# Reordering the hand-written entry of a one-core mixer-trunk kernel

## Chip, core and metric

The kernel runs on one core of one Trainium2 chip. The metric is device time in microseconds (us) of one execution. The core has five engines, each of which takes its own instructions in order: TensorE (PE) multiplies matrices, VectorE (DVE), ScalarE (ACT) and GpSimd (POOL) work elementwise, and SyncE (SP) here only issues DMAs. Matmuls write to PSUM, of which the kernel uses eight banks of 128 x 512 float32; in this kernel DVE and ACT read and write it, and POOL works on SBUF alone.

## The reference

One layer over 1024 positions of width 1024, in float32:

```
h = rmsnorm(x) * norm_g ;  p = h @ w_in            # w_in: 1024 x 6656
u,v,z_a, x_b,b_g,c_g,z_b, x_c,z_c, g_a,g_b,g_c = split(p)
a = gelu(u) * (chunkwise causal mix of layernorm(gelu(v))) * silu(z_a)
b = b_g * conv3(c_g * x_b) * silu(z_b)
c = (multi-scale causal mean of x_c - x_c) @ w_pool * pool_scale * silu(z_c)
m = sigmoid(g_a) * (a @ w_pa) + sigmoid(g_b) * (b @ w_pb) + sigmoid(g_c) * (c @ w_pc)
out = rmsnorm(x + m @ w_o) * final_g
```

## The kernel before

**Precision.** Every float32 operand of a matmul is split in two: `hi` is the operand rounded by an ACT copy (names end in h, or ch for weights), `lo` is the rest, by a subtraction on DVE or POOL (S1l, cl). A product is three matmuls per 128 rows: hi·hi, hi·lo, lo·hi (`mm3`).

**Seven products for eight.** After the entry, the projection runs over pairs of weight units. h (transposed) is cut in four blocks A11, A12, A21, A22, a pair of units in B11, B12, B21, B22, and each pair costs seven products of 12 matmuls instead of eight:

```
PRODUCTS = (("A11", "B11"), ("A12", "B21"), ("S2", "T2"), ("S3", "T3"),
            ("S1", "T1"), ("A22", "T4"), ("S4", "B22"))
```

S1 = A21 + A22, S2 = S1 - A11, S3 = A11 - A21, S4 = A12 - S2 are made once, in the entry. T1 = B12 - B11, T2 = B22 - T1, T3 = B22 - B12, T4 = B21 - T2 are made for each pair, on DVE into a PSUM bank. A "step" n is one product; `prep(n)` makes its T (if it has one) and its ch and cl. Steps 0 to 3 are the *early products* A11·B11 and A12·B21 of pairs 0 and 1; steps 4 to 8 are S1·T1, S2·T2, S3·T3, A22·T4 and S4·B22 of pair 0; step 9 begins pair 1. A result tile of step n is p with the number n. A product begins by preparing weights up to `AHEAD = 6` steps ahead. From pair 2 on a part of every second pair is done by a further level of the same scheme (`joint`, tiles T_j and cj), whose left side `cut_again` makes from A12 during pair 0.

**The entry** (from line 482) computes the mean squares of x (`squares`, `sums`, `power`, and `newton`, called `roots`), the columns v of the projection from x that is not yet normalised (`project_v`, eight rows i of 24 matmuls each over k), `gelu_v` with the root as a scale, and then the normalised blocks A and S. `as_row` transposes the roots on PE, so that `scaled` can multiply x by them. Rows 0 to 3 of v are computed k by k, since the weights are still arriving; rows 4 to 7 one after the other. `gelu_v` also writes gv to DRAM; `stats_v(i)` takes its mean and variance by bn_stats on DVE, from gv itself or (`again`) from a copy gw reloaded by SP.

**What sets the order.** The entry stands in a block of manual schedule: there PE, ACT, DVE and POOL run its lines in the order in which they are written. All that follows is ordered by the compiler's list planner, with the order of the program as priority and its own costs; it may put instructions from behind the block between its lines. Slots are handed out per tag, eight PSUM banks (`ps`), three of `T` (gv, gw, T_j), 18 of `wc` (ch, cl and the weights of v), four of `raw`; a tile waits until the slot's last tile was read. `keep_s1(p)` copies the first early product of pair p out of PSUM on ACT, `first_o0(p)` adds that to the second early product on DVE and runs a sigmoid on ACT, and both free a bank. p4 (S1·T1) is given a bank after T1 to T4 of pair 0 and T1, T2 of pair 1. S4·B22 is accumulated onto p4 and so waits until DVE has read p4 (u2, u3, o1 in the main loop).

Of the kernel before, what the change touches and what calls it, by code (L numbers as in the profile page):

```python
# [18 lines left out]
KH = KT // 2  # L19
# [42 lines left out]
def hybrid_layer(ctx: ExitStack, tc: tile.TileContext, x, xt, units, ws, wpool, small, rows, out):  # L62
# [128 lines left out]
    def x_lo(half, kk):  # L191
        for c in range(2):
            k = kk + KH * c
            hi, lo = (z[:, kk, :] for z in hb[XB[2 * half + c]])
            nc.vector.scalar_tensor_tensor(out=lo, in0=xs[half, kk][c], scalar=ng[:, k:k + 1], in1=hi.bitcast(F32),
                                           op0=ALU.mult, op1=ALU.subtract)
# [29 lines left out]
    def roots(half):  # L226
        newton(*root[half], norms[:, 1, KH * half:KH * half + KH])

    def as_row(half):
        for i in range(KH):  # L230
            e = KH * half + i
            nc.tensor.transpose(out=B[6 + half][:, tsl(i)], in_=norms[:, 1, e:e + 1].to_broadcast([P, P]), identity=ident)
# [19 lines left out]
    def project_v(i, k, terms=range(3)):  # L252
        hi, lo = (z[:, k % KH, tsl(i % KH)] for z in hb[XB[2 * (i // KH) + k // KH]])
        w = wv[k]
        for e in terms:
            nc.tensor.matmul(pv[i], lhsT=(hi, hi, lo)[e], rhs=(w[0], w[1], w[0])[e], start=k == 0 and e == 0,
                             stop=k == KT - 1 and e == 2)

    def gelu_v(i):
        gvs[i] = slot("T", f"gv{i}", (P, CW))  # L260
        nc.scalar.activation(out=gvs[i], in_=pv[i], func=AF.Gelu_apprx_tanh, scale=norms[:, 1, i:i + 1])
        nc.sync.dma_start(out=v_dram[:, i, :], in_=gvs[i])
# [47 lines left out]
            raw[u] = slot("raw", f"raw{u}", (P, 2, HALF))  # L310
            nc.sync.dma_start(out=raw[u], in_=units[u])

    def prep(n):
        kind, p, r = steps[n]
        name = PRODUCTS[r][1]
        u0, u1 = pairs[p][2]
        load_raw(u0)
        if kind == "n":
            load_raw(u1)
            b = {"B11": raw[u0][:, 0, :], "B21": raw[u0][:, 1, :], "B12": raw[u1][:, 0, :], "B22": raw[u1][:, 1, :]}  # L320
        else:
            v0 = pairs[p + 1][2][0]
            load_raw(v0)
            b = {"B11": raw[u0][:, 1, 0:256], "B21": raw[u0][:, 1, 256:], "B12": raw[v0][:, 1, 0:256],
                 "B22": raw[v0][:, 1, 256:]}

        def add(name, i0, i1, into=None):
            if kind == "n":
                t = bank(f"{name}_{kind}{p}")
            else:  # L330
                t = slot("T", f"{name}_{kind}{p}", (P, HALF)) if into is None else into
            if kind == "j" and into is None:
                T[kind, p, name, "rest"] = t[:, 256:]
                t = t[:, 0:256]
            tt(nc.vector if kind == "n" else nc.gpsimd, t, b[i0] if i0 in b else T[kind, p, i0], b[i1] if i1 in b else T[kind, p, i1], ALU.subtract)
            T[kind, p, name] = t

        if r == 4 and kind == "n":
            add("T1", "B12", "B11")
        elif r == 2:  # L340
            if kind == "j":
                add("T1", "B12", "B11")
            add("T2", "B22", "T1", T["j", p, "T1", "rest"] if kind == "j" else None)
        elif r == 3:
            add("T3", "B22", "B12")
        elif r == 5:
            add("T4", "B21", "T2", T["j", p, "T3", "rest"] if kind == "j" else None)
        if kind == "n":
            hi = slot("wc", f"ch{n}", (P, HALF), F32R)
            lo = slot("wc", f"cl{n}", (P, HALF), F32R)  # L350
            if name in b:
                split_to(hi, lo, b[name], nc.gpsimd)
            else:
                split_to(hi, lo, T[kind, p, name])
            comb[n] = (hi, lo)
        elif r == 0:
            hi = slot("wc", f"ch{n}", (P, HALF), F32R)
            lo = slot("wc", f"cl{n}", (P, HALF), F32R)
            split_to(hi, lo, raw[u0][:, 1, :])
            comb[n] = (hi[:, 0:256], lo[:, 0:256])  # L360
            comb[steps.index(("j", p, 1))] = (hi[:, 256:], lo[:, 256:])
        elif r > 1:
            w = slot("wc", f"cj{n}", (P, 2, 256), F32R)
            split_to(w[:, 0, :], w[:, 1, :], b[name] if name in b else T[kind, p, name])
            comb[n] = (w[:, 0, :], w[:, 1, :])
# [116 lines left out]
    with tc.manual_schedule(engines={ET.PE, ET.Activation, ET.DVE, ET.Pool}):  # L482
        x_hi(0, 0)
        w_hi(0)
        x_lo(0, 0)
        w_lo(0)
        w_lo(4)
        squares(0, 0)
        x_hi(0, 1)
        x_lo(0, 1)  # L490
        w_hi(1)
        w_lo(1)
        w_lo(5)
        squares(0, 1)
        x_hi(0, 2)
        x_lo(0, 2)
        squares(0, 2)
        squares(0, 3)
        w_hi(2)
        x_hi(0, 3)  # L500
        w_hi(3)
        w_lo(2)
        for e in range(3):
            for i in range(KH):
                project_v(i, 0, [e])
        for k in (4, 1):
            for i in range(KH):
                project_v(i, k)
        for i in range(2):
            project_v(i, 5)  # L510
        sums(0)
        w_lo(6)
        w_lo(3)
        w_lo(7)
        x_lo(0, 3)
        roots(0)
        for i in range(2, KH):
            project_v(i, 5)
        for i in range(KH):
            project_v(i, 2)  # L520
        as_row(0)
        for kk in range(KH):
            squares(1, kk)
        for kk in range(KH):
            x_hi(1, kk)
        for i in range(KH):
            project_v(i, 6)
        for i in range(KH):
            project_v(i, 3)
        sums(1)  # L530
        for kk in range(2):
            x_lo(1, kk)
        roots(1)
        for kk in range(2, KH):
            x_lo(1, kk)
        for i in range(KH):
            project_v(i, 7)
            if i == 2:
                as_row(1)
        prep(0)  # L540
        for i in range(KH):
            gelu_v(i)
        for kk in range(KH):
            scaled(0, kk)
            split_h(kk, ("A11", "A12"))
        for k in KORDER:
            project_v(4, k)
        gelu_v(4)
        for kk in range(KH):
            scaled(1, kk)  # L550
        for k in KORDER:
            project_v(5, k)
        gelu_v(5)
        for i in range(6, NT):
            for k in KORDER:
                project_v(i, k)
        f11, f12 = ([xs[0, kk][c] for kk in range(KH)] for c in range(2))
        f21, f22 = ([xs[1, kk][c] for kk in range(KH)] for c in range(2))
        for kk in range(KH):
            s1_, s2_ = (B[6 + c - 2 * (kk % 2)] for c in range(2))  # L560
            tt(nc.vector, s1_, f21[kk], f22[kk], ALU.add)
            tt(nc.vector, s2_, s1_, f11[kk], ALU.subtract)
            tt(nc.vector, f12[kk], f12[kk], s2_, ALU.subtract)
            split_s("S1", kk, s1_)
            split_s("S2", kk, s2_)
            if kk == 1:
                gelu_v(6)
        for n in range(1, 4):
            prep(n)
        gelu_v(7)  # L570
        early_product(0, 0)
        early_product(0, 1)
        early_product(1, 0)
        early_product(1, 1)
        prep(4)
        for kk in range(KH):
            split_h(kk, ("A22",))
        prep(5)
        split_s("S4", 0, f12[0])
        keep_s1(0)  # L580
        for kk in range(1, KH):
            split_s("S4", kk, f12[kk])
        at = [B[6 + kk % 2] for kk in range(KH)]
        for kk in range(KH):
            tt(nc.vector, at[kk], f11[kk], f21[kk], ALU.subtract)
            if kk:
                split_s("S3", kk - 1, at[kk - 1])
            else:
                first_o0(0)
        split_s("S3", 3, at[3])  # L590
        keep_s1(1)
        for n in range(6, 9):
            prep(n)
        first_o0(1)
    prepped[0] = 9

    lr = const.tile([P, NT], F32, name="lr")
# [101 lines left out]
    for p, (kind, j, _) in enumerate(pairs):  # L699
# [21 lines left out]
            block(p, o0, lohalf, px, both[p], f0, kind)  # L721
        py_ = product(("n", 4), more=True)
        then(4)
        if p == 0:
            for i in (5, 6, 7):
                stats_v(i, False)
        if late is not None and nxt[0] is not None and not (kind == "g" and j >= 6):
            late()
            late = None
# [19 lines left out]
            late = None  # L749
        block(p, o1, lohalf, product(("n", 6), py_), u2, f1, kind)  # L750
        then(6)
        if p == 0:
            for i in range(5):
                stats_v(i)
        elif p == 1:
            v_norm()

        if kind == "g":
# [343 lines left out]
```

## Time and profile before

| | |
|---|---|
| median of 3 runs | 862.29 us (861.37 to 862.78) |
| the profiled execution | 862.83 us, of which the span of instructions is 861.1 us |
| mean granted TensorE clock | 0.980 |
| busy | PE 819.4 us (95%), DVE 644.8 (75%), POOL 384.3 (45%), ACT 365.1 (42%) |

All rows come from the profiled execution; times in them count from its first instruction. The share of the span is an average over stages; the windows below show the entry (to about 92 us), the first pairs, and the long middle. A matmul's end is modelled and overlaps the next one's start, so the spacing of starts is what one costs. An idle time in brackets is put down to the instruction whose semaphore came last.

### The profile page before, as it was taken

To read this page: it belongs to the slowest core of one execution; us is meant where nothing else is said; L and a number is where in the kernel's file an instruction comes from. 1 tells how busy PE (TensorE), PEld (TensorE's weight loads), DVE (VectorE), ACT (ScalarE), POOL (GpSimd) and SP (SyncE) were. 2 spreads that over 40 slices of the span, in tenths; PEclk is the share of its full clock that TensorE was granted. 3 is DMA by queue.
4 is the path that set the end of the run, shared out by engine and by line. 5 is a ranking of instruction groups with operands and counts; after the bars stand their busy time and mean duration, and the time that the engine had idled before them with its cause. 6 is when DMAs were issued, how large, how long until landed. Compare 5 with 4: busy or idle time off the path is not lost. (4 is left out here: it accounts for less than half of the span.)

```text
span 861.1 us, 11050 instructions
## 1 busy us (share of the span) xinstructions
PE 819.4 (95%) x3828; PEld 682.3 (79%) x3828; DVE 644.8 (75%) x1034; ACT 365.1 (42%) x721; POOL 384.3 (45%) x366
## 2 busy tenths in 40 slices
PE   9895889999999999999999999999999999998894
PEld 7674778888888888888888888888878888785684
DVE  5897797776777777868787777878565725897996
ACT  7735264646454333323236353535342401354431
POOL 5334337575665535444451223142000543648864
PEclk9997899999999999999999999999999999999998
DMA  8210434332513202122121413314497633421132
GB/s 343 98 37 13 135 122 135 110 137 73 168 65 123 96 28 98 49 74 97 49 77 50 150 61 114 122 53 147 154 382 270 229 114 121 148 74 51 49 147 98
DMA packets 34599, 100.34 MB, mean 117 GB/s; under 512 B 3568, under 2 KB 9712, under 8 KB 34544
## 3 DMA queue, kind: packets, MB, share of 16 engines
q1 hardware_dynamic: 28928, 85.21, 28.3%
q10 hardware_dynamic: 5616, 14.44, 4.6%
q8 instruction: 30, 0.49, 0.2%
q14 instruction: 25, 0.20, 0.1%
HBM read 74.47 MB, written 25.17 MB: 116 GB/s over the span
## 5 line engine op out<-in xcount | busy, mean ns | idle before, releaser
L82 POOL TENSOR_TENSOR cl<-raw,ch 128x512 fp32r<-128x512 f32 x58 | 82.2, 1421 | 147.9 <-ACT ch L85 65.3
L82 DVE TENSOR_TENSOR cl<-T_n,ch 128x512 fp32r<-128x512 f32 x112 | 76.4, 683 | 56.0 <-PE p L90 42.6
L85 ACT CAST ch<-T_n 128x512 fp32r<-128x512 f32 x112 | 65.5, 585 | 113.0 <-DVE T_n L82 64.3
L82 DVE TENSOR_TENSOR o<-p,u 128x512 f32<-128x512 f32 x84 | 57.1, 683 | 24.3 <-PE p L91 24.1
L85 ACT CAST ch<-raw 128x512 fp32r<-128x512 f32 x71 | 43.8, 620 | 55.9 <-PE p L90 49.3
L89 PE MATMUL p<-S1h,ch 128*128 128x512 f32 x112 | 44.9, 401 | 8.5 <-ACT s L458 8.5
L89 PE MATMUL p<-S4h,ch 128*128 128x512 f32 x112 | 44.8, 400 | 3.2 <-DVE o L82 2.6
L82 DVE TENSOR_TENSOR p<-p,p 128x256 f32<-128x256 f32 x78 | 32.4, 416 | 18.2 <-PE p L91 18.0
L91 PE MATMUL p<-A22h,cl 128*128 128x512 f32 x112 | 44.2, 394 | 1.8 <-DVE cl L82 1.8
L90 PE MATMUL p<-S1l,ch 128*128 128x512 f32 x112 | 44.7, 399 | 0.0
L91 PE MATMUL p<-S1h,cl 128*128 128x512 f32 x112 | 44.5, 398 | 0.0
L89 PE MATMUL p<-S2h,ch 128*128 128x512 f32 x112 | 44.3, 396 | 0.0
L90 PE MATMUL p<-A22l,ch 128*128 128x512 f32 x112 | 44.1, 394 | 0.0
L91 PE MATMUL p<-S4h,cl 128*128 128x512 f32 x112 | 44.1, 393 | 0.0
L90 PE MATMUL p<-S4l,ch 128*128 128x512 f32 x112 | 44.1, 393 | 0.0
L89 PE MATMUL p<-A22h,ch 128*128 128x512 f32 x112 | 44.0, 393 | 0.0
L90 PE MATMUL p<-S2l,ch 128*128 128x512 f32 x112 | 43.8, 391 | 0.0
L89 PE MATMUL p<-A11h,ch 128*128 128x512 f32 x112 | 43.7, 391 | 0.0
L90 PE MATMUL p<-A11l,ch 128*128 128x512 f32 x112 | 43.7, 390 | 0.0
L89 PE MATMUL p<-S3h,ch 128*128 128x512 f32 x112 | 43.7, 390 | 0.0
L90 PE MATMUL p<-S3l,ch 128*128 128x512 f32 x112 | 43.7, 390 | 0.0
L91 PE MATMUL p<-S2h,cl 128*128 128x512 f32 x112 | 43.6, 389 | 0.0
(485 smaller groups left out, 2525.5 us busy)
## 6 DMA issues: line engine op xcount, KB each, us to landing
raw<-in_units_dram SPq DMA_DIRECT2D x56, 512.0 KB, 3.3
gate<-o ACTq DMA_DIRECT2D x24, 512.0 KB, 3.3
gt<-gate SPq DMA_DIRECT2D x24, 512.0 KB, 4.4
rawp<-in_units_dram SPq DMA_DIRECT2D x12, 512.0 KB, 4.5
yr<-y SPq DMA_DIRECT2D x12, 512.0 KB, 5.1
y<-o SPq DMA_DIRECT2D x8, 512.0 KB, 2.9
rawo<-in_units_dram SPq DMA_DIRECT2D x8, 512.0 KB, 3.8
res<-in_x_dram SPq DMA_DIRECT2D x8, 512.0 KB, 3.3
```

The source lines that it names most:

```text
L82: eng.tensor_tensor(out=o, in0=a, in1=b, op=op)
L85: nc.scalar.copy(out=hi, in_=src)
L89: nc.tensor.matmul(ps, lhsT=wh, rhs=bh, start=first, stop=False, skip_group_check=shared)
L90: nc.tensor.matmul(ps, lhsT=wh, rhs=bl, start=False, stop=False, skip_group_check=shared)
L91: nc.tensor.matmul(ps, lhsT=wl, rhs=bh, start=False, stop=last, skip_group_check=shared)
```

## The change

Lines of the entry are moved; no arithmetic of the result is changed.

- **Roots.** `roots(0)` and `as_row(0)` move behind the projections k = 2, 6 and 3 of rows 0 to 3 and, for `as_row(0)`, behind `sums(1)`; the squares of the second half move ahead of them. `as_row(1)` moves into row 4, behind its fifth k. One `x_lo(1, 0)` moves ahead of `sums(1)`, the others stay ahead of `roots(1)`.
- **Early weights.** `prep(1)` moves between rounds 1 and 2 of the S1/S2 loop, `prep(2)` and `prep(3)` behind round 2's splits; they stood behind the loop.
- **Twos.** `prep` gets a mode that makes only the T, so that T1 and T2 are computed one after the other before either is rounded, and T3 and T4 likewise. T1 and T2 now stand behind the A22 splits. `prep(8)` moves to the end.
- **Copies.** `keep_s1(1)` moves ahead of the last S3 split; `first_o0(0)` and the S4 splits move from before the S3 splits (and within them) to behind T4, in turns.
- **Statistics.** `stats_v` of rows 5 to 7 moves from the middle of pair 0 to the end of the entry, that of rows 0 to 4 from the end of pair 0 to behind pair 1's first product.

```diff
+    summed = set()
+
+    def prep(n, only_sum=False):
...
-        if r == 4 and kind == "n":
+        if n in summed:
+            pass
+        elif r == 4 and kind == "n":
             add("T1", "B12", "B11")
...
+        summed.add(n)
+        if only_sum:
+            return
...
         x_lo(0, 3)
-        roots(0)
         for i in range(2, KH):
             project_v(i, 5)
-        for i in range(KH):
-            project_v(i, 2)
-        as_row(0)
         for kk in range(KH):
             squares(1, kk)
         for kk in range(KH):
             x_hi(1, kk)
-        for i in range(KH):
-            project_v(i, 6)
-        for i in range(KH):
-            project_v(i, 3)
+        for k in (2, 6, 3):
+            for i in range(KH):
+                project_v(i, k)
+        roots(0)
+        x_lo(1, 0)
         sums(1)
-        for kk in range(2):
+        as_row(0)
+        for kk in range(1, KH):
             x_lo(1, kk)
         roots(1)
-        for kk in range(2, KH):
-            x_lo(1, kk)
         for i in range(KH):
             project_v(i, 7)
-            if i == 2:
-                as_row(1)
         prep(0)
...
         for k in KORDER:
             project_v(4, k)
+            if k == KORDER[4]:
+                as_row(1)
...
             if kk == 1:
                 gelu_v(6)
-        for n in range(1, 4):
-            prep(n)
+                prep(1)
+            elif kk == 2:
+                prep(2)
+                prep(3)
         gelu_v(7)
         early_product(0, 0)
         early_product(0, 1)
         early_product(1, 0)
         early_product(1, 1)
-        prep(4)
         for kk in range(KH):
             split_h(kk, ("A22",))
+        prep(4, True)
+        prep(5, True)
+        prep(4)
         prep(5)
-        split_s("S4", 0, f12[0])
         keep_s1(0)
-        for kk in range(1, KH):
-            split_s("S4", kk, f12[kk])
         at = [B[6 + kk % 2] for kk in range(KH)]
         for kk in range(KH):
             tt(nc.vector, at[kk], f11[kk], f21[kk], ALU.subtract)
             if kk:
                 split_s("S3", kk - 1, at[kk - 1])
-            else:
-                first_o0(0)
+        keep_s1(1)
         split_s("S3", 3, at[3])
-        keep_s1(1)
-        for n in range(6, 9):
-            prep(n)
+        prep(6, True)
+        prep(7, True)
+        prep(6)
+        prep(7)
+        split_s("S4", 0, f12[0])
+        first_o0(0)
+        split_s("S4", 1, f12[1])
         first_o0(1)
+        for kk in range(2, KH):
+            split_s("S4", kk, f12[kk])
+        prep(8)
+        for i in (5, 6, 7):
+            stats_v(i, False)
...
         then(4)
-        if p == 0:
-            for i in (5, 6, 7):
-                stats_v(i, False)
+        if p == 1:
+            for i in range(5):
+                stats_v(i)
...
         then(6)
-        if p == 0:
-            for i in range(5):
-                stats_v(i)
-        elif p == 1:
+        if p == 1:
             v_norm()
```

## Rows read from the trace of the kernel before

**Rows 1.** Windows: each engine's busy us (instructions), granted clock, DMA share, GB/s.
```profile
17.00:59.50 42.50, 38.62 (x174) 31.68 (x175) 38.49 (x61) 24.68 (x42) 18.85 (x15) 0.96 0.28 101
59.50:75.00 15.50, 13.26 (x49) 9.82 (x48) 11.79 (x17) 9.37 (x18) 9.73 (x7) 0.89 0.05 17
75.00:83.40 8.40, 0.03 (x1) 0.03 (x1) 6.24 (x10) 4.54 (x7) 0.00 (x0) 0.75 0.00 0
83.40:103.40 20.00, 17.58 (x65) 13.97 (x65) 13.95 (x28) 4.50 (x8) 4.18 (x5) 0.84 0.45 145
103.40:125.40 22.00, 19.78 (x83) 16.00 (x84) 21.19 (x32) 11.07 (x24) 10.04 (x7) 0.85 0.27 96
...
150.00:800.00 650.00, 643.46 (x3072) 538.98 (x3071) 473.23 (x734) 265.24 (x517) 280.14 (x239) 1.00 0.33 115
```

**Rows 2.** Timeline of PE, 23 to 116 us: start, us, line, operation, idle before.
```profile
23.73 0.65 PE L232 MATMUL entry<-ident,norms 128*128 128x128 f32 x4 [1.55 <-DVE norms L82]
...
35.18 1.11 PE L232 MATMUL entry<-ident,norms 128*128 128x128 f32 x4 [2.33 <-DVE norms L82]
...
59.56 0.39 PE L89 MATMUL p<-A11h,ch 128*128 128x512 f32 x1
...
63.88 0.50 PE L89 MATMUL p<-A12h,ch 128*128 128x512 f32 x1 [1.44 <-ACT ch L85]
...
65.65 0.63 PE L89 MATMUL p<-A12h,ch 128*128 128x512 f32 x1
...
68.21 0.63 PE L89 MATMUL p<-A12h,ch 128*128 128x512 f32 x1
...
69.22 0.39 PE L89 MATMUL p<-A11h,ch 128*128 128x512 f32 x1
...
71.95 0.39 PE L89 MATMUL p<-A12h,ch 128*128 128x512 f32 x1
...
83.37 0.79 PE L89 MATMUL p<-S1h,ch 128*128 128x512 f32 x1 [8.55 <-ACT s L458]
...
103.39 0.80 PE L89 MATMUL p<-S4h,ch 128*128 128x512 f32 x1 [2.42 <-DVE o L82]
...
115.28 0.50 PE L91 MATMUL p<-A22h,cl 128*128 128x512 f32 x1 [1.77 <-DVE cl L82]
```

**Rows 3.** Timeline of DVE in the entry.
```profile
19.75 2.50 DVE L82 TENSOR_TENSOR tmp<-tmp 128x4 f32<-128x4 f32 x2 [0.26 <-POOL tmp L82]
...
23.59 5.46 DVE L82 TENSOR_TENSOR acc<-entry,acc 128x512 f32<-128x512 f32 x7
...
33.42 0.35 DVE L82 TENSOR_TENSOR tmp<-tmp 128x4 f32<-128x4 f32 x2
...
37.70 10.61 DVE L239 SCALAR_TENSOR_TENSOR x<-x,sm,entry 128x512 f32<-128x512 f32 x16
48.23 1.58 DVE L82 TENSOR_TENSOR entry<-x 128x512 f32<-128x512 f32 x1
...
83.47 0.69 DVE L82 TENSOR_TENSOR T_n<-raw 128x512 f32<-128x512 f32 x1
```

**Rows 4.** Groups of DVE instructions, 63 to 92 us: count, busy us, mean ns, idle before.
```profile
L82 DVE TENSOR_TENSOR cl<-T_n,ch 128x512 fp32r<-128x512 f32 x7 | 4.7, 689 | 2.7 <-ACT ch L85 2.6
L82 DVE TENSOR_TENSOR S4l<-x,S4h 128x512 fp32r<-128x512 f32 x4 | 4.6, 1219 | 0.0
```

**Rows 5.** Timeline of POOL beside them.
```profile
68.27 5.51 POOL L82 TENSOR_TENSOR A22l<-x,A22h 128x512 fp32r<-128x512 f32 x4
```

**Rows 6.** Timeline of ACT, 77 to 83 us.
```profile
77.03 1.28 ACT L472 ACT_TABLE_LOAD   x1 [4.23 <-DVE o L82]
...
82.73 0.59 ACT L458 COPY s<-p 128x512 f32<-128x512 f32 x1
```

**Rows 7.** Groups of DVE instructions, 92 to 126 us.
```profile
L270 DVE BATCH_NORM_STATS2 stats<-gw 128x6 f32<-128x512 f32 x5 | 3.4, 692 | 5.3 <-DMA gw<-v_dram 5.3
...
L82 DVE TENSOR_TENSOR tmp<-tmp 128x8 f32<-128x8 f32 x2 | 2.5, 1232 | 0.6 <-POOL tmp L82 0.6
```

More of the change, by code (lines that the diff above doesn't have):

```diff
@@ L311, in load_raw @@
             nc.sync.dma_start(out=raw[u], in_=units[u])
-    def prep(n):
+    summed = set()
+    def prep(n, only_sum=False):
         kind, p, r = steps[n]
```

## The prediction

> **What bounds the kernel now.** I read the windows by stage first, then TensorE's timeline through the entry, then the timelines of VectorE (DVE), ScalarE (ACT) and GpSimd (POOL) at the places where TensorE (PE) waits. From 150 to 800 us PE is busy 643.46 of 650 us at full clock [rows 1]: there nothing but matmuls counts, and a microsecond won earlier is a microsecond at the end. Between 17 and 125.4 us PE is idle 3.88 + 2.24 + 8.37 + 2.42 + 2.22 = 19.1 us, and the granted clock is below 1.00 in every one of these windows, in stretches at the lower level of 1.2 GHz. One such microsecond does half the work, so it costs half of itself. The 17 to 59.5 window (0.96) holds 3.4 us of it, 59.5 to 75 (0.89) 3.4, 83.4 to 103.4 (0.84) 6.4, 103.4 to 125.4 (0.85) 6.6.
>
> The waits have names [rows 2]: 1.55 and 2.33 us for the roots of the rows (norms), 1.44 for the rounded weights of the second early product (ch, and shortly after it cl), 8.55 before S1·T1, put down to ACT's copy s, 2.42 before S4·B22 for DVE's o, 1.77 inside A22·T4 of the second pair for DVE's cl. So the change works on a stage that PE does bound, and its worth is how many of these go. At full clock a product of 12 matmuls takes 71.95 − 69.22 = 2.73 us, 0.227 a matmul; at half clock six take 68.21 − 65.65 = 2.56, 0.427 each [rows 2].
>
> **Step A, the roots.** roots(0), four small DVE instructions, stands today between POOL's last low parts of the weights. Two of the four took 2.50 us there and 0.35 elsewhere [rows 3], and as_row(0) on PE waits for the last. Moved behind three more blocks of projections (k = 2, 6, 3), its input is ready long before. DVE's seven adds of squares can start when the first square stands in PSUM, at about 20.3 instead of 23.59 [rows 3], and at the old pace (5.46 for seven) end at 25.8; roots(0) is then some 0.65 (twice 0.35) and ends at 26.4. PE reaches sums(1) at 27.5 and as_row(0) at 28.3: no wait, 1.7 us to spare. After sums(1) DVE still has three pairs of x_lo (six at 0.66, from scaled's 10.61 for 16) and roots(1): done at 33.1. as_row(1) now stands after five of the eight k of row 4, at PE's 34.8: no wait, 1.7 us again. PE's work from 17.8 to the first early product is 150 matmuls at 0.227 (34.0) and 1.6 for sums and transposes: it starts at 53.5 instead of 59.56. **6.0 us**: the 3.88 of idle and what restarts and half clock took. DVE starts scaled at about 33.1 instead of 37.70, 4.6 us earlier.
>
> **Step B, early weights between sums.** prep(1) moves between rounds 1 and 2 of the S1/S2 sums, prep(2) and prep(3) behind round 2. Their slots come free with the first matmuls of row 7 (53.5 − 24 × 0.227 = 48.1), ACT waits there for DVE anyhow, and POOL is idle. The loop starts 4.6 us before its 48.23 [rows 3], at 43.6, and a quarter of its old 15.8 us is 4, so ch1/cl1 are there by about 53 and the others by 58; PE needs them at 56.2, 59.0 and 61.7. The four early products then run without a gap: 4 × 2.73 = 10.9, to 64.4, where they took from 59.56 to 71.95 + 2.73 = 74.7. **4.2 us more**: idle 2.24, the rest half clock. The cost lies on DVE. The first sum of a round has both inputs in SBUF, and the one such sum that ran beside POOL took 1.58 instead of about 0.68 [rows 3]. Rounds 2 and 3 now have POOL beside them: 2 × 0.9 = 1.8 us. The two bn_stats that ran in this loop leave it (1.7), so it takes its old 15.8 (48.23 to 64.0) and ends at 59.5.
>
> Here a rule speaks against the change. The low parts S4l, both inputs in SBUF, took 1219 ns in the mean [rows 4] beside POOL's A22l of 5.51 / 4 = 1.38 us each [rows 5]; cl, with one input in PSUM, took 689 [rows 4]. The Trainium skill ("SBUF — State Buffer", section "Who interferes with whom") says that a VectorE instruction with two SBUF inputs and a GpSimd instruction that reads SBUF exclude each other, the later one waiting for the whole of the other. The trace agrees. By that rule the loop could lose two whole POOL instructions, 2.8 us instead of 1.8, and S4l, moved behind A22l's end, gains about 2.
>
> **Step C, twos and copies.** After the loop DVE has T1, T2, cl4, cl5, four differences and four S3l before T3: 12 × 0.66 = 7.9, and about 1.2 waiting for ACT, which now rounds A22 before T1. T3 comes at 68.6 instead of 83.47 [rows 3], because S4l (4.6) and first_o0(0) with its table load (1.28) [rows 6] no longer stand before it. p4's wait ended with the copy keep_s1(1) at 82.73 + 0.6 [rows 6], since p4 writes the bank that p2 held. That copy moves ahead of the last S3h on ACT, two DVE instructions before T3, to about 67. Which bank p4 gets is not in the trace; it can be the one that the last S3l frees, 68.6. I take 67.5: PE waits 67.5 − 64.4 = 3.1 instead of 8.55 (**5.4 us**). Bounds: 0 if its bank is one that keep_s1(0) freed, 7 if first_o0(0) frees it. Behind the wait of 1.44 the matmuls ran at 0.427 [rows 2], so behind one of 3.1 I leave a stretch of 3.4 us, as in the first two windows (1.7 lost), instead of the 6.4 of the window behind 83.4, of which about 6.0 under p4 and p5 (3.0 lost): **1.3 us**. Together PE is 16.9 us earlier in the products behind p4.
>
> **Step D, what is late next.** DVE at T3 is 83.47 − 68.6 = 14.9 earlier, but now has behind it what it used to have ahead: four S4l (2.6), one first_o0 (0.7), three bn_stats with aggregates (2.6), and about 2 us (1.28 + 0.63) waiting while ACT loads its table and runs the sigmoid between S4h parts; behind that wait stand S4l and the next pair's T and cl, and of these PE needs the cl first. Its lead shrinks to 14.9 − 7.9 = 7.0. Against that, after 92 it sat idle 5.3 us for reloaded rows gw [rows 7], standing in front of the sums u and o on which S4·B22 waits, and two of v_norm's small instructions took 2.5 us, some 2.1 too long by the same measure as in roots(0), a third one about 1 too long. The last three bn_stats now hold their slots to about 80, so reloads come later and u and o go first; v_norm shifts behind cut_again's roundings. If all of that is regained DVE's lead is 7.0 + 5.3 + 3.1 = 15.4. The reload itself (five DMAs on SP's queue, behind the raw loads) moves from pair 0 to pair 1, and v_norm's first reader stands a pair later: hidden. The leads of 16.9 on PE and 15.4 on DVE meet: I take 16.3, nearer PE's, since PE has no need of v_norm so early. The bounds: 7.0, every old wait coming again, and 16.9 + 2.42 + 1.77 + 3.3 + 0.2 = 24.6, PE never waiting again.
>
> The profiled execution took 862.83, 0.5 above the median of 862.29. 862.8 − 16.3 = 846.5; against the median **846.0**.
>
> **Rivals.**
> - *DVE becomes the bound* (855.3). For: 21.19 of 22 us busy from 103.4 to 125.4 [rows 1], and it takes on 5.9 us behind T3. Against: its idle and slowed time there was not work. Gain 7.0.
> - *PE runs free* (837.7). For: all roundings of weights are prepared six products ahead. Against: the same 21.19 of 22. Gain 24.6.
> - *Slower: PE at half clock.* If the entry hands PE each product a little late, the clock stays at 1.2 GHz from the first early product to p7, and a product takes 5.1 instead of 2.73: 2.4 each. From seven such products the gain is gone; with eight (19.0) the time is 864.9. For: 6.4 us of the window behind 83.4 ran so. Against: weights of the early products are ready microseconds ahead.
> - *The change does not do what it says*: instructions from behind the written block may be placed between its lines by the planner, as bn_stats was, and fill the freed DVE time with the wrong ones; with p4's wait staying at 8.55 and steps C and D empty, the gain is A and B, all lost again at p4: 862.
>
> **Numbers.** Forecast (841 to 851) 0.55; DVE bound (851 to 857) 0.18; PE free (836 to 841) 0.19; change without effect 0.03; half clock 0.05. The range 838 to 855 leaves out the last two (0.08), a third of the DVE case (0.06) and a quarter of the free one (0.05). A measurement of this kernel can tell about 0.2% (1.7 us) from no change: faster 0.92, same 0.03, slower 0.05, from the first three cases, the fourth and the fifth.
>
> **What would show it.** A: no idle before the L232 transposes, first early product at 53 to 54. B: no gap inside the four early products, clock 1.00 to their end, S4l back at 0.7. C: first S1·T1 at 66 to 69; its releaser names the bank. D: S4·B22 of pair 0 about 16 us earlier, reloads behind u and o. Wrong would be: p4 at 72 or later (the bank), or a new idle of over 5 us between 75 and 110 with DVE as releaser; or the gain there but lost between 125 and 150.

## The result, and the profile after

The kernel after took 852.34 to 854.26 us, median 852.94, beside 862.53 for the kernel before on the same chip: a ratio of 0.9891 [0.9868, 0.9914]. (A fourth run took 1646.63 us, for a reason that no trace here shows, and is left out of these.) The profiled execution took 854.26 with a span of 852.6, 8.57 less than the one of before. Forecast was 846.0, with a range of 838 to 855: the direction and the range hold, and of the forecast gain of 16.3 us some 7 to 8 are missing (9.6 were measured by the medians, 8.57 by the profiled executions). The time lies outside the forecast's own 841 to 851 (chance 0.55) and inside the 851 to 857 of the rival in which DVE becomes the bound (0.18).

The windows of the kernel after, in the same stretches as [rows 1]:

```profile
17.00:59.50 42.50, 42.32 (x199) 35.34 (x199) 38.31 (x62) 27.41 (x47) 23.67 (x18) 1.00 0.28 103
59.50:75.00 15.50, 8.91 (x33) 6.96 (x32) 14.17 (x21) 10.31 (x19) 5.47 (x4) 0.75 0.11 38
75.00:83.40 8.40, 8.40 (x34) 6.79 (x32) 5.98 (x12) 4.86 (x10) 1.30 (x1) 0.85 0.13 36
83.40:103.40 20.00, 13.79 (x55) 10.98 (x54) 17.05 (x30) 5.24 (x11) 10.24 (x9) 0.83 0.42 140
103.40:125.40 22.00, 19.53 (x97) 16.55 (x96) 17.44 (x34) 13.61 (x30) 7.34 (x7) 0.92 0.55 175
...
150.00:800.00 650.00, 643.76 (x3072) 539.50 (x3071) 479.26 (x746) 263.47 (x514) 281.58 (x249) 1.00 0.32 113
```

The first window is now full and at full clock. Of the 19.1 us in which PE was idle, 0.18 + 6.59 + 6.21 + 2.47 = 15.45 are left, and they have names again. PE's timeline, answering to [rows 2]:

```profile
54.08 0.39 PE L89 MATMUL p<-A11h,ch 128*128 128x512 f32 x1
...
64.28 0.39 PE L89 MATMUL p<-A12h,ch 128*128 128x512 f32 x1
71.71 0.77 PE L89 MATMUL p<-S1h,ch 128*128 128x512 f32 x1 [6.59 <-DVE S3l L82]
73.13 0.63 PE L89 MATMUL p<-S1h,ch 128*128 128x512 f32 x1
...
76.97 0.63 PE L89 MATMUL p<-S2h,ch 128*128 128x512 f32 x1
77.93 0.39 PE L89 MATMUL p<-S2h,ch 128*128 128x512 f32 x1
...
94.99 0.80 PE L89 MATMUL p<-S4h,ch 128*128 128x512 f32 x1 [6.21 <-DVE o L82]
...
111.77 0.76 PE L89 MATMUL p<-S4h,ch 128*128 128x512 f32 x1 [2.47 <-DVE o L82]
```

Read it by leads over [rows 2]. The first early product starts 59.56 − 54.08 = 5.5 us earlier, S1·T1 11.7 (83.37 − 71.71), S4·B22 of the first pair 8.4 (103.39 − 94.99), and 8.5 is left at the end. So 3.3 us are lost between S1·T1 and S4·B22, where PE's wait grew from 2.42 to 6.21. DVE's timeline shows what stands there:

```profile
87.27 0.69 DVE L270 BATCH_NORM_STATS2 stats<-gw 128x6 f32<-128x512 f32 x1 [0.31 <-DMA gw<-v_dram]
88.13 0.69 DVE L270 BATCH_NORM_STATS2 stats<-gw 128x6 f32<-128x512 f32 x1 [0.17 <-DMA gw<-v_dram]
...
88.96 0.67 DVE L82 TENSOR_TENSOR u<-p,s 128x512 f32<-128x512 f32 x1
92.07 1.33 DVE L270 BATCH_NORM_STATS2 stats<-gw 128x6 f32<-128x512 f32 x2 [2.44 <-DMA gw<-v_dram]
...
93.53 0.67 DVE L82 TENSOR_TENSOR u<-p,u 128x512 f32<-128x512 f32 x1
94.24 0.69 DVE L82 TENSOR_TENSOR o<-p,u 128x512 f32<-128x512 f32 x1
```

Two statistics of reloaded rows stand in DVE's queue in front of the first u, two more in front of the second u and of o, and these waited 2.44 us for their DMAs. They are the stats<-gw of [rows 7]: of the wait that the prediction thought would go, 0.31 + 0.17 + 2.44 = 2.9 of 5.3 us are still there, and four of the five statistics, where all five stood before, are still in front of o.

### The profile page after: what moved, and what is told of

Same layout as the page of the kernel before. It is cut to its first block, busy times and chain, and to the rows that moved or that the text cites. A ratio compares the mean times of both kernels' runs of the same rounds, so it can differ in the third digit from the quotient of the medians.

```text
span 852.6 us, 11052 instructions
## 1 busy us (share of the span) xinstructions
PE 814.5 (96%) x3828; PEld 680.2 (80%) x3828; DVE 641.0 (75%) x1034; ACT 365.6 (43%) x721; POOL 383.0 (45%) x366
## 5 line engine op out<-in xcount | busy, mean ns | idle before, releaser
L85 ACT CAST cj<-T_j 128x256 fp32r<-128x256 f32 x52 | 20.9, 403 | 55.3 <-PE p L90 42.4
L91 PE MATMUL p<-S2h,cl 128*128 128x512 f32 x112 | 43.6, 389 | 0.0
```

The costliest lines, as they stand in the source:

```text
L85: nc.scalar.copy(out=hi, in_=src)
L91: nc.tensor.matmul(ps, lhsT=wl, rhs=bh, start=False, stop=last, skip_group_check=shared)
```

## The experiments

All ratios are to the kernel before, timed on the same chip as the kernel beside it, with 95% intervals. "p0" is the start of the first early product, "S1·T1" and "S4·B22" are the starts of these products of the first pair, all from PE's timeline of each kernel:

| kernel | p0 | S1·T1 | S4·B22 | ratio |
|---|---|---|---|---|
| before | 59.56 | 83.37 | 103.39 | 1 |
| roots only | 53.71 | 79.84 | 99.21 | 0.9948 |
| all but the roots | 59.76 | 74.86 | 99.94 | 0.9939 |
| after | 54.08 | 71.71 | 94.99 | 0.9891 |
| statistics in old places | 53.76 | 72.33 | 96.37 | 0.9890 |
| A22 later | 53.70 | 69.57 | 94.66 | 0.9911 |
| first product earlier | 53.66 | 64.54 | 93.20 | 0.9871 |
| rows not reloaded | 53.71 | 71.36 | 92.35 | 0.9857 |
| two products earlier | 53.67 | 64.55 | 90.44 | 0.9843 |
| before, without reload | 59.52 | 81.61 | 97.84 | 0.9878 |
| all three | 53.74 | 64.62 | 89.90 | 0.9835 |
| no reload, A22 in the loop | 53.66 | 64.54 | 87.33 | 0.9830 |
| no reload, norm in gaps | 53.83 | 71.84 | 87.75 | 0.9818 |
| no reload, S4 together | 53.64 | 64.52 | 85.56 | 0.9786 |

The ratio follows the column of S4·B22 far more than that of S1·T1, though not strictly: the kernel before without reload has a better ratio than three kernels whose S4·B22 comes earlier.

**The parts of the change.** First the roots alone in the kernel before, then all of the change but the roots, then the kernel after with its statistics where they were.

```diff
+        for k in (2, 6, 3):
+            for i in range(KH):
+                project_v(i, k)
+        roots(0)
+        x_lo(1, 0)
         sums(1)
+        as_row(0)
...
+            if k == KORDER[4]:
+                as_row(1)
```

> The kernel before with the first part of the change alone: roots and rows of roots later, as_row(1) inside row 4. Theory 1 (VectorE's lead is what lasts): the first early product starts near 53.4 instead of 59.56, but the second one still waits for weights rounded behind VectorE's S1/S2 loop, and that loop starts only as much earlier as scaled does, 37.70 to about 34.6; so 3.1 us of the 6 last: 0.9964 of before. Theory 2 (TensorE's lead lasts): 6 us less, 0.993. Theory 3: nothing lasts, 1.000.

Measured 858.55, 0.9948 [0.9935, 0.9961]. PE's timeline:

```profile
60.37 0.79 PE L89 MATMUL p<-A12h,ch 128*128 128x512 f32 x1 [3.78 <-ACT ch L85]
...
79.84 0.80 PE L89 MATMUL p<-S1h,ch 128*128 128x512 f32 x1 [7.99 <-ACT s L458]
```

The 5.9 us won at p0 are partly given back at once: the wait for the second early weights grows from 1.44 to 3.78, and 3.5 reach S1·T1. That is theory 1's mechanism; the ratio lies between the two theories (0.9964 and 0.993), and theory 1's is just outside the interval.

> The changed kernel with the roots and their rows put back where they stood before; early weights, twos, copies and statistics stay moved. Theory 1: what is left of the 8.9 us is 8.9 less the 3.1 of the roots, 5.8 us, 0.9933 of before. Theory 2: 8.9 less 6, 2.9 us, 0.9966. If roots give nothing: 0.989.

Measured 857.16, 0.9939 [0.9926, 0.9953]. The two parts, 0.52% and 0.61%, sum to 1.13%, and the whole gave 1.09%: within the intervals they add, and neither needs the other. That is theory 1 (0.9933).

```diff
-        for i in (5, 6, 7):
-            stats_v(i, False)
...
-        if p == 1:
-            for i in range(5):
-                stats_v(i)
+        if p == 0:
+            for i in (5, 6, 7):
+                stats_v(i, False)
...
-        if p == 1:
+        if p == 0:
+            for i in range(5):
+                stats_v(i)
+        elif p == 1:
             v_norm()
```

> The changed kernel with both moves of statistics undone: rows 5 to 7 after the second product of pair 0, rows 0 to 4 at the end of pair 0. Theory 1 (the same work on VectorE, and the reloads stand in front of u and o either way): S1·T1 up to 2 us later, the end within 1 us of the changed kernel, 0.988 to 0.990 of before. Rival (the move of the statistics carries part of the gain): 3 us or more slower than the changed kernel, 0.9925 or above.

Measured 853.55, 0.9890 [0.9875, 0.9905]: where the statistics are written carries none of the gain, and none of the loss. DVE's timeline shows something more:

```profile
86.76 1.50 DVE L270 BATCH_NORM_STATS2 stats<-gw 128x6 f32<-128x512 f32 x2 [0.73 <-DMA gw<-v_dram]
...
91.65 1.29 DVE L270 BATCH_NORM_STATS2 stats<-gw 128x6 f32<-128x512 f32 x2 [2.58 <-DMA gw<-v_dram]
...
95.03 0.69 DVE L270 BATCH_NORM_STATS2 stats<-gw 128x6 f32<-128x512 f32 x1 [1.29 <-DMA gw<-v_dram]
95.64 0.67 DVE L82 TENSOR_TENSOR o<-p,u 128x512 f32<-128x512 f32 x1
```

Here the statistics of rows 5 to 7 ran long before, among the S1/S2 sums, and DVE is ready for the reloaded rows at 86.03 instead of 86.96. Yet it waits 4.6 us for them instead of 2.9, and o, behind all five here, comes 1.4 us later than in the kernel after. So the rows held DVE there, not the work ahead of them.

**The reload.** First the five reloaded rows and their statistics are left out, with a constant in place of each mean and variance.

```diff
+    nc.gpsimd.memset(mv, 1.0)
...
-            for i in range(5):
-                stats_v(i)
+            pass
```

> The changed kernel without the five reloads of gv and their statistics: mean and variance of rows 0 to 4 are the constant 1, the rest is computed as before. Theory 1 (VectorE, in its order, holds u and o behind the reloaded rows): the wait of 6.2 us before S4·B22 of pair 0 falls to 2 or less with the half-clock stretch behind it, and 4 to 6 us are won against the changed kernel: 0.983 of before. Rival (VectorE is simply full there, or v_norm takes the place of the statistics): under 1.5 us, 0.988 to 0.989.

Measured 850.47, 0.9857 [0.9842, 0.9871], between the two theories. DVE's timeline says why:

```profile
87.51 0.68 DVE L82 TENSOR_TENSOR u<-p,s 128x512 f32<-128x512 f32 x1
89.99 0.37 DVE L82 TENSOR_TENSOR tmp<-tmp 128x8 f32<-128x8 f32 x2 [1.81 <-POOL tmp L82]
...
91.61 0.69 DVE L82 TENSOR_TENSOR o<-p,u 128x512 f32<-128x512 f32 x1
```

With the rows gone, v_norm's small instructions moved up in front of the second u and of o and waited 1.81 us for POOL's power. So the next run takes the reload and the eight statistics off DVE altogether, and writes v_norm by hand where DVE waits for ACT anyway:

```diff
-        nc.scalar.activation(out=gvs[i], in_=pv[i], func=AF.Gelu_apprx_tanh, scale=norms[:, 1, i:i + 1])
+        nc.scalar.activation(out=gvs[i], in_=pv[i], func=AF.Gelu_apprx_tanh, scale=norms[:, 1, i:i + 1],
+                             accum_out=mv[:, i, 0:1])
...
+        nc.scalar.activation(out=pv[i], in_=gvs[i], func=AF.Square, accum_out=mv[:, i, 1:2])
...
         first_o0(0)
...
+        late_v = power(v, 1.0, LN_EPS, (2, slice(0, NT)))
         split_s("S4", 1, f12[1])
         first_o0(1)
+        newton(*late_v, lr)
```

> This kernel computes all of the reference. Mean and variance of v come from running sums that ACT's Gelu and a Square pass give along (8 more ACT passes), so no row is read back, no bn_stats stands on DVE, and v_norm's small instructions are written into the two gaps of 1.2 us in which DVE waits for ACT between the S4 roundings. Theory 1 (the 6.21 us before S4·B22 are DVE standing at the reloaded rows, with u and o queued behind): that wait falls under 2 us, S4·B22 of pair 0 starts at 87.5 to 89 instead of 94.99, ratio 0.980 to 0.983 of the kernel before. Rival (DVE's own instructions behind T3 set that product, the reload only fills its idle time): S4·B22 stays above 93 and the ratio at 0.987 to 0.990. The run without the reload, 0.9857, lay between because v_norm's wait for POOL took the place of the rows.

Measured 846.46, 0.9818 [0.9799, 0.9836]. DVE's timeline, and then PE's:

```profile
85.48 0.68 DVE L82 TENSOR_TENSOR u<-p,s 128x512 f32<-128x512 f32 x1
...
87.00 0.69 DVE L82 TENSOR_TENSOR o<-p,u 128x512 f32<-128x512 f32 x1
```

```profile
71.84 0.77 PE L89 MATMUL p<-S1h,ch 128*128 128x512 f32 x1 [6.97 <-DVE S3l L82]
...
87.75 0.50 PE L89 MATMUL p<-S4h,ch 128*128 128x512 f32 x1
...
104.53 0.47 PE L89 MATMUL p<-S4h,ch 128*128 128x512 f32 x1 [3.00 <-DVE o L82]
```

S1·T1 starts as late as in the kernel after, and the wait before S4·B22 is gone entirely. Theory 1's numbers came out, but the run takes more off DVE than the rows' wait: of what stood in front of o in the kernel after, seven statistics with their aggregates were 7 × (0.69 + 0.17) = 6.0 us of work, and 2.9 were idle; v_norm's instructions take some of it back. The run before parts them in an estimate. Without v_norm between the two u (88.19 to 90.89) its o would have come 2.7 us earlier, at 88.9; so the rows with their own statistics are worth some 5.3 of the 7.24 us by which o comes earlier (94.24 to 87.00), the three other statistics some 1.9. Below, "without the reload" stands for all that this edit takes off DVE.

The same edit in the kernel before, with the same sums on ACT, asks how much of this belongs to the change:

```diff
                 first_o0(0)
...
+                late_v = power(v, 1.0, LN_EPS, (2, slice(0, NT)))
         split_s("S3", 3, at[3])
...
+        newton(*late_v, lr)
...
         first_o0(1)
...
-            for i in (5, 6, 7):
-                stats_v(i, False)
...
-            for i in range(5):
-                stats_v(i)
```

> This is the kernel before with the edit of the run without reload: mean and variance from sums that ACT gives along, v_norm's small instructions written behind first_o0(0) and before first_o0(1); it computes all of the reference. Theory 1 (the reload became the late thing only when the entry got shorter; in the kernel before S1·T1 comes so late that the rows are nearly there): the 2.42 us before S4·B22 and at most the 1.77 behind it go, less up to 1.6 for ACT's longer passes ahead of the early weights: ratio 0.994 to 1.000. Rival (the reload costs the kernel before the 7 to 8 us too, so that the change itself is worth no more than was measured): 0.990 to 0.992 or less.

Measured 852.43, 0.9878 [0.9864, 0.9891]. My theory fell: the reload and the statistics on DVE together cost the kernel before 1.2%, more than they cost the kernel after (0.9891 to 0.9818, 0.7%). The two windows that answer to those of [rows 1], and then the stretch behind S1·T1, from its start to 92 us, first in the kernel before and then in this one:

```profile
83.40:103.40 20.00, 20.00 (x84) 16.36 (x83) 18.89 (x29) 8.51 (x16) 11.32 (x9) 0.94 0.30 106
103.40:125.40 22.00, 21.96 (x117) 18.83 (x116) 16.37 (x28) 12.97 (x29) 5.03 (x5) 1.00 0.58 180
```

```profile
83.37:92.00 8.63, 8.63 (x26) 6.88 (x27) 7.88 (x14) 4.50 (x8) 1.28 (x1) 0.65 0.46 148
...
81.61:92.00 10.39, 10.39 (x37) 8.39 (x38) 9.58 (x19) 4.50 (x8) 3.08 (x4) 0.79 0.29 101
```

I had counted only the waits. They are 2.42 + 2.22 = 4.6 us of idle. But behind them the granted clock also rises, from 0.85 to 1.00 in the second window: 6.6 us at the lower level are gone, worth half of that, 3.3. Behind S1·T1 it rises from 0.65 to 0.79, from 6.0 us at the lower level to 4.4, worth 0.8; that stretch follows S1·T1's own wait, which this run still has. And S1·T1 comes 1.8 earlier, since the statistics no longer stand in and behind the S1/S2 sums. Together 10.5, and the spans differ by 861.1 − 849.9 = 11.2; 0.7 stay unexplained. So without the reload the change is worth 0.9878 − 0.9818 = 0.6%, some 5 us. Its lead is 9.8 at S1·T1 and 10.1 at S4·B22; then the kernel without reload waits 0.53 and 3.00 us for DVE, where the kernel before without reload waits no more.

**The bank and A22.** S1·T1 waits 6.59 us for the PSUM bank that the last S3l frees. Written into the entry, it gets another one:

```diff
         keep_s1(1)
+        early_product(0, 4)
         split_s("S3", 3, at[3])
```

> S1·T1 of pair 0 is written into the entry behind the second copy s, so it takes a PSUM bank that T1 frees and not the one that the last S3 difference frees. Both theories: it starts at 67 to 69 instead of 71.71, as the forecast had it. Theory 1 (the reloaded rows set S4·B22): the start of S4·B22 moves only as far as the rows and their order on DVE allow; of the 3 to 4 us won some 1 to 3 stay, ratio 0.9855 to 0.988, and the wait before S4·B22 is above 5 us still. Rival (the chain of products from S1·T1 sets the end): all 4 us stay, ratio 0.984 to 0.985, the wait at S4·B22 shorter than 5.

Measured 851.48, 0.9871 [0.9851, 0.9890]. S1·T1 started at 64.54, without any wait, earlier than I expected. PE's and DVE's timelines:

```profile
73.67 0.80 PE L89 MATMUL p<-S2h,ch 128*128 128x512 f32 x1 [6.25 <-DVE cl L82]
...
93.20 0.80 PE L89 MATMUL p<-S4h,ch 128*128 128x512 f32 x1 [5.37 <-DVE o L82]
```

```profile
90.61 0.69 DVE L270 BATCH_NORM_STATS2 stats<-gw 128x6 f32<-128x512 f32 x1 [2.75 <-DMA gw<-v_dram]
91.22 0.68 DVE L82 TENSOR_TENSOR u<-p,u 128x512 f32<-128x512 f32 x1
```

The wait moved on to S2·T2, whose bank is now the one that cl frees, and S4·B22 still waits 5.37 for o, in front of which DVE waits 2.75 for a row: 7.2 us at S1·T1 become 1.8 at S4·B22. By the ratio and by that wait this is theory 1. With both products in the entry (ahead_of_turn issues one as early_product does, and product then returns its bank):

```diff
         keep_s1(1)
+        ahead_of_turn(4)
+        ahead_of_turn(2)
         split_s("S3", 3, at[3])
```

> The kernel after with S1·T1 and S2·T2 of pair 0 both written into the entry behind the second copy s, so that both get banks that T1 and the first copy s free; in the run with S1·T1 alone S2·T2 took T3's bank and waited 6.25 us for it. Both theories: S1·T1 at 67 to 69, S2·T2 behind it without a wait, the products of S3 and A22 from 74 on. Theory 1 (reloaded rows in front of u and o set S4·B22): PE gains some 3 us there and waits them again at S4·B22; ratio 0.985 to 0.989. Rival (PE's late start sets the end): 0.981 to 0.984.

Measured 849.15, 0.9843 [0.9829, 0.9857]: a little better than theory 1 allowed, at the edge of the rival. It doesn't decide between them, since the planner, with the first products earlier, also put both u in front of all five rows and o in front of four of them, and DVE waits for none: S4·B22 waits 2.12 and starts at 90.44.

```diff
-        for kk in range(KH):
-            split_h(kk, ("A22",))
         prep(4, True)
...
         prep(7)
+        for kk in range(KH):
+            split_h(kk, ("A22",))
         split_s("S4", 0, f12[0])
```

> The rounding of A22 on ACT and POOL moves from before T1/T2 to behind T3/T4. Both theories: DVE's wait of 1.1 us for ch goes and the two differences that took 1.16 and 1.75 us beside POOL's A22l take 0.7, so S1·T1 starts 2 to 3 us earlier, at 69 to 70; S4l runs beside POOL now and takes 1.2 instead of 0.68 a piece. Theory 1 (the reloaded rows set S4·B22): none or at most 1 us of it is seen at the end, ratio 0.988 to 0.990. Rival (the start of S1·T1 sets the end): ratio 0.985 to 0.987. Slower than 0.990 if S4l's longer time or a late A22l for A22·T4 counts.

Measured 854.95, 0.9911 [0.9894, 0.9929]. S1·T1 starts 2.1 us earlier and S4·B22 0.3; at the end nothing of it is left. That is theory 1, with the cost of S4l on top: the first two took 1.04 and 1.15 us.

> This kernel computes all of the reference. The three edits together: no reload and v_norm in the gaps, S1·T1 written into the entry, A22 rounded behind T3/T4. Theory 1: with the reload gone the start of S1·T1 counts again, up to the point where DVE's own work behind T3 holds S4·B22: ratio 0.976 to 0.981, S4·B22 of pair 0 at 83 to 87. Rival (DVE's own work sets that product whatever stands before it): no better than the kernel without the reload alone.

Measured 848.13, 0.9835 [0.9817, 0.9853]: a miss. It is no better than the kernel without reload alone, as the rival had it. DVE's timeline:

```profile
73.73 1.04 DVE L82 TENSOR_TENSOR S4l<-x,S4h 128x512 fp32r<-128x512 f32 x1 [1.51 <-ACT S4h L85]
...
75.29 0.64 DVE L606 TENSOR_SCALAR mv<-mv 128x8 f32<-128x8 f32 x1
75.97 1.20 DVE L82 TENSOR_TENSOR lb<-mv 128x8 f32<-128x8 f32 x1
77.20 0.17 DVE L608 SCALAR_TENSOR_TENSOR mv<-mv,lb 128x8 f32<-128x8 f32 x1
...
80.60 2.39 DVE L82 TENSOR_TENSOR S4l<-x,S4h 128x512 fp32r<-128x512 f32 x2
...
87.65 0.68 DVE L82 TENSOR_TENSOR u<-p,s 128x512 f32<-128x512 f32 x1
```

S4l waits for ACT, which rounds A22 first, and runs beside POOL; S2·T2, too, waits 4.18 for a bank. DVE comes to u 2.2 us later than without this part (85.48), though it began T3 2.5 us earlier.

**What is late next.** A22 moved into the last round of the S1/S2 sums instead, with the two products in the entry and no reload:

```diff
                 prep(2)
                 prep(3)
+                split_h(0, ("A22",))
+                split_h(1, ("A22",))
+        split_h(2, ("A22",))
+        split_h(3, ("A22",))
         gelu_v(7)
```

> This kernel computes all of the reference. The run without reload (0.9818) with S1·T1 and S2·T2 written into the entry and A22's rounding moved into the last round of the S1/S2 sums, where ACT waits for DVE. Theory: DVE's wait for ch before the S3 differences (1.76 us) falls to about 1 and the slow differences (1.16 and 1.75) to about 0.7 and 1.2, so T3 comes 1 to 2.5 us earlier, at 69 to 70.5, and with it u, o and S4·B22, since DVE's own instructions set that product now: ratio 0.977 to 0.980. Rival (POOL beside the last round slows its sums as much as it speeds the differences, and an earlier PE waits at o): 0.9805 to 0.983.

Measured 848.02, 0.9830 [0.9815, 0.9846]: the rival by the ratio, though T3 did come earlier, at 70.03, as the theory had it. What that won is lost behind T3: DVE still waits between the S4l's for ACT's table load and sigmoids (1.85 and 0.38), and POOL's second-level weights wait until 88.04 for raw ones. So the last run writes the S4 roundings together:

```diff
-        split_s("S4", 0, f12[0])
-        first_o0(0)
-        split_s("S4", 1, f12[1])
-        first_o0(1)
-        for kk in range(2, KH):
...
+        for kk in range(KH):
             split_s("S4", kk, f12[kk])
         prep(8)
...
+        first_o0(0)
+        first_o0(1)
+        newton(*late_v, lr)
```

> This kernel computes all of the reference. The kernel of the run with A22 in the loop (no reload, S1·T1 and S2·T2 written into the entry; 0.983), with the four roundings of S4 written together ahead of the two first sums o0 and their sigmoids, so that DVE doesn't wait for ACT's table load and sigmoids between S4l's (1.85 and 0.38 us in that run). Theory (DVE's instructions from T3 to u, o set S4·B22): DVE comes to o 1.5 to 2.5 us earlier, S4·B22 of pair 0 at 85 to 86.5 instead of 87.33, ratio 0.9785 to 0.982. Rival (what sets the end behind S4·B22 is the cutting of the second level and the raw weights for it, which waited until 88.04 there): the ratio stays at 0.982 to 0.985, whatever S4·B22 does; then the run without reload alone stays the fastest.

Measured 841.94, 0.9786 [0.9765, 0.9806], the fastest of all. DVE's timeline, and one window:

```profile
74.30 2.50 DVE L82 TENSOR_TENSOR S4l<-x,S4h 128x512 fp32r<-128x512 f32 x4
...
84.07 0.68 DVE L82 TENSOR_TENSOR o<-p,u 128x512 f32<-128x512 f32 x1
```

```profile
83.40:103.40 20.00, 16.95 (x81) 13.58 (x80) 19.27 (x30) 10.43 (x22) 11.17 (x8) 1.00 0.37 124
```

The four S4l follow each other without a gap, o comes 2.5 us earlier than in the run before (86.59), S4·B22 starts at 85.56 without a wait, and the clock stays at 1.00. The rival's ratio did not come, but its cause is not excluded: POOL's second-level weights, too, came earlier in this run, at 81.39 instead of 88.04.

## Why the prediction was right or wrong

**Steps A and B were right.** p0 at 54.08 was forecast for 53.5; the two waits for norms are gone; the four early products run without a gap from there, a product each 2.72 us, to 65.0 (forecast 64.4). The costs on DVE, answering to [rows 3]:

```profile
30.88 1.78 DVE L195 SCALAR_TENSOR_TENSOR S4l<-x,sm,S4h 128x512 fp32r<-128x512 f32 x1
...
34.57 10.61 DVE L239 SCALAR_TENSOR_TENSOR x<-x,sm,entry 128x512 f32<-128x512 f32 x16
...
56.41 1.81 DVE L82 TENSOR_TENSOR entry<-x,x 128x512 f32<-128x512 f32 x1
...
64.74 2.83 DVE L82 TENSOR_TENSOR entry<-x,x 128x512 f32<-128x512 f32 x2
...
71.48 0.69 DVE L82 TENSOR_TENSOR T_n<-raw 128x512 f32<-128x512 f32 x1
```

One x_lo took 1.78 us instead of 0.75 beside POOL's first cl; that is 1.0 of the 1.5 us by which scaled starts later, at 34.57 and not at 33.1. Of the sums beside POOL I had put two at 2 × 0.9; one was slow (1.81).

**Step C: the mechanism was right, its sizes were off.** "T3 comes at 68.6": it came at 71.48. Of the 2.9, 1.5 were already missing at the start of the S1/S2 loop (45.10 for 43.6), and 1.5 is the pair of differences that now runs beside POOL's A22l, 2.83 for two instead of 1.3. For S1·T1's bank I had named two candidates and took the earlier one (67.5); it was the other one, the bank of the last S3l, at 71.5. The wait was 6.59 instead of 3.1, near the bound of 7. Behind it the matmuls run at 0.427 each until 77.5, 5.8 us at the lower level, where I had 3.4. So the "1.3 us" of clock were not won.

**Step D failed**, in one sentence: "the last three bn_stats now hold their slots to about 80, so reloads come later and u and o go first". The slots were held to 85, but the reloads came earlier, not later. SP's issues of them, first in the kernel before, then in the kernel after (first and last start):

```profile
L269 SPq DMA_DIRECT2D gw<-v_dram x5: 319/319/373, 89.1 to 98.7; - x5
...
L269 SPq DMA_DIRECT2D gw<-v_dram x5: 319/320/327, 83.9 to 92.8; - x5
```

And u and o don't go first: the order on DVE is fixed by the planner before anything runs, and it put four statistics in front of o although they are written behind it; by what reckoning, no run shows. So DVE's lead at S4·B22 is 8.4, near the lower bound of 7.0 ("every old wait coming again"). Of the 5.3 us of waiting for rows, only 2.4 were regained. The 3.1 of v_norm could not move S4·B22 of pair 0 at all: that product started at 103.39 in the kernel before, and v_norm's slow instructions stood behind it:

```profile
108.67 2.50 DVE L82 TENSOR_TENSOR tmp<-tmp 128x8 f32<-128x8 f32 x2 [0.57 <-POOL tmp L82]
```

The prediction had named this as a sign of being wrong, "a new idle of over 5 us between 75 and 110 with DVE as releaser", and it came: 6.21 us before S4·B22. That the range held is owed to the bound of 7.0 in it, not to step D.

With the rows and all statistics off DVE, the same entry gives S4·B22 a lead of 103.39 − 87.75 = 15.6 and a time of 846.46, beside the forecast's 15.4 and 846.0. That this agrees is luck, not a proof of the sum 7.0 + 5.3 + 3.1: the run also takes the three statistics of rows 5 to 7 off DVE, 2.6 us that the forecast had counted against the lead, and its T3 comes 3.0 us later than forecast (71.61 for 68.6).

The rule of the Trainium skill ("SBUF — State Buffer", section "Who interferes with whom") agrees with these traces: each slow instruction of 128 x 512 above has two SBUF inputs and a GpSimd instruction beside it. S4l, moved behind A22l's end, took 0.68 each, as forecast [rows 4], and 1.04 where A22l stood beside it again. I had used the rule on the loop and on S4l, and not on the differences that came to stand in S4l's place.

**The rivals.** DVE as the bound came nearest, more by the reloaded rows and their statistics than by the rest of its work. PE did not run free, the half clock did not take the gain, and the planner did place statistics between u and o, which I had priced only as a change without effect.

## What to carry to other kernels

When an entry gets shorter, ask of each in-order queue what stands in front of the instruction that the next product needs, and don't let a wait that the change doesn't touch vanish from the sum: here four of five rows that are read back kept their place in the queue in front of o, although they were issued some 5 us earlier. A wait in front of a matmul stream costs more than its length, since the stretch behind it runs at the lower clock: here 4.6 us of idle carried 3.3 us more. And where work with two SBUF inputs leaves GpSimd's side, look at what takes its place there.

## What the runs showed of the hardware

Small instructions can pay for a neighbour nearly as much as large ones: in the run of all three parts, two of v_norm's with 8 columns took 0.64 and 1.20 us while POOL made A22l, and the next one, alone, 0.17. A sum taken along with an activation costs ACT a second entry of 0.19 us, as the run without reload has it for each of its 16 passes. In that run the granted clock reads 0.94 from 150 to 800 us:

```profile
150.00:800.00 650.00, 641.96 (x3043) 537.45 (x3042) 480.78 (x751) 262.46 (x519) 288.10 (x257) 0.94 0.33 114
```

Yet three matmuls take 0.68 us there at 300 us, as in the kernel after at 1.00, and the span is the second shortest of all. So a mean clock a little under 1.00 over a long stretch need not be time lost; what it stands for stays open.
